# Three up-projection output pairs of phase 0 as two by two steps of seven products

## The chip, the cores and the metric

The kernel runs on one core of one Trainium2 chip. The metric is the time of one execution on the device in microseconds (us), as the median of several runs. Profile times count from the first instruction of the span.

## The reference, cut to what matters

One block of a streaming encoder on x of 512 positions by 1024 channels. The part that the change touches is the channel mixer after the merge:

```python
x = x + (g_conv * y_conv + g_attn * y_attn) @ w_o[l]     # output projection
h = rms_norm(x, norm_ffn_g[l])
up = causal_dwconv(h @ w_up[l], conv_ffn_w[l])           # 1024 -> 2 * 2816
a, b = jnp.split(up, 2, axis=-1)
x = x + (jax.nn.silu(a) * b) @ w_down[l]                 # 2816 -> 1024
```

All operands are float32.

## The kernel before, in words

**Layout and products.** Activations lie transposed, 128 channels on the partitions and the 512 positions along the free axis, so x is 8 blocks of 128 by 512. A weight block is 128 by 128. Each float32 operand is kept as a high part in the type fp32r and a low part, the difference. A product of a weight block and an activation block is three matmul passes (high by high, low by high, high by low), each cut into two halves of 256 positions: six matmuls (`mm3`, whose line is L290). For a chunk of weights, ACT writes the high part (L259) and DVE the low part (L263); both have two buffers (`wh`, `wl`), so a chunk can be split as soon as the chunk before the last one is used up.

**Steps of seven products.** For some matrices the kernel takes two output blocks, two input blocks and the two halves of the positions as a two by two product of blocks, with seven block products where eight would do it the plain way (Winograd's form of Strassen's scheme). Sums of weight blocks and sums of activation blocks ("forms") go in, and four PSUM banks hold the seven products, which are then merged. `seven` runs them, and its matmuls have the line L308. A step of two such doubles takes two chunks: P (768 columns of plain weights, 18 matmuls) and F (1024 columns of weight sums, 24 matmuls). Before the change this is done for five pairs of gates (`GATES`) and for the down projection (`STEPS`).

**Weight sums.** `make_forms` builds the F chunks in device memory, with DMAs alone: copies on SP's queue (L198) and accumulating DMAs on POOL's queue (L201), one wave after another by the calls of `slot()` that the stages make. For the down projection of phase 0 there are six groups, first copied at the start of the output projection.

**Stages.** Projections with attention; gates and merge (`yc`, `ya`, mix chunks, `GATES`), which leaves `mh`/`ml`; output projection (8 chunks `wo0` to `wo7`), whose evacuation adds x (`xr`, 8 DMAs on POOL's queue, L1011 and L1012), scales and splits the sum into `x1h`/`x1l` (L1013, L1014) and adds its squares into `ssq2` on POOL (L966); phase 0 of the channel mixer with the output pairs j = 0 to 11 (`up`, chunks `up0` to `up23`, two per pair), then its steps of the down projection; phase 1 with pairs 12 to 21 and their steps; the last rows and the final norm.

**An up pair.** Two blocks of 48 matmuls, each in one PSUM bank of a ring of six. The norm's factor `rb` is not in `x1h`/`x1l`; it is multiplied in at the evacuation (L1046), since the norm of the whole position is known only after `wo7`. So the matmuls of `up0` and `up1` (`lead`) run ahead of it, with the norm's reduction (`pc_n`) and broadcast (`pb_n`) placed between them. Then come three taps of the convolution (L543 on ACT, L544 and L547 on DVE), silu (L1056, ACT) and the product of the pair (POOL, `ge` at L1061 for even j and `go` at L1068 for odd j). After each odd pair DVE and ACT make the activation forms for the down projection (L1078 to L1088).

**What sets the order.** Matmuls and the listed DMAs keep the order of the program (`keep`). Weight chunks are a single list, `stream`; SP's queue loads them in that order, up to `LOOK` = 7 ahead, into four buffers `raw` (F chunks into `rf`, or into `rg` in the gate stage) as buffers come free. SP's queue is in order: a load that waits holds back all behind it. Work of DVE and ACT that can be put off stands in the list `later`, and after each split `run_later` takes as much of it as a budget in us, set by the chunk's kind, allows.

Of the kernel before, what the change touches and what calls it, by code (L numbers as in the profile page):

```python
# [61 lines left out]
DOUBLES = GATES + STEPS[0] + STEPS[1]  # L62
GROUPS = {"gate": (2, 4, 1), 0: (2, 4, 1), 1: (2, 3, 1)}
# [3 lines left out]
def block_kernel(ctx, tc, xT, vecs, wv, win, wmix, wo, wup, wst, wdp, outT):  # L67
# [168 lines left out]

    def split(hl=None):
# [30 lines left out]
        parts.append((hi, lo))  # L268
        run_later(k, {"u": 1.7, "P": 1.6, "F": 0.75, "i": 3.0, "m": 3.0, "d": 0 if nm == "dp1" else 2.1}.get(nm[0], 3.5))
# [498 lines left out]
    def seven(doubles, n0, sets, operand, goes_on=None, stays=None, done=None):  # L768
# [3 lines left out]
        for n, d in enumerate(doubles):  # L772
            for kind in "PF":
                prods = []
                for s_, (i, q) in enumerate(d):
                    for f, g, b, h in PROD:
                        if (f < 3) == (kind == "P"):
                            wants.setdefault(f"{kind}{n0 + n}", []).append(("q", q))
                            c = 3 * s_ + f if f < 3 else s_ + len(d) * (f - 3)
                            prods.append((c, i, operand(q, g), b, h))  # L780
# [31 lines left out]

    mg = ExitStack()
    mp = mg.enter_context(tc.tile_pool(name="mp", bufs=1))
    pools["rg"] = mp
    mh = mp.tile([P, KB, S], F32R, tag="mh", name="mh")
    ml = mp.tile([P, KB, S], F32R, tag="ml", name="ml")
# [105 lines left out]

    for j in range(KB):
        gs = []
        if j == 0:
# [11 lines left out]
        for pp, hh, ll, o in ((yc, ych, ycl, 0), (ya, oth, otl, 4)):  # L938
            for k in range(4):
# [12 lines left out]
    x1 = xp.tile([P, KB, S], F32, tag="x1", name="x1")  # L952
# [49 lines left out]

    po = None
    make_forms(len(GATES), len(GATES) + len(STEPS[0]), 0)
    for j in range(KB):
# [12 lines left out]
        square_into(ssq2, x1[:, j, :], j == 0, mp, f"sq2_{j}")  # L1018
    mg.close()
    ab.close()  # L1020
# [4 lines left out]
    fp.tile([P, PADL], F32, tag="pad", name="pad_f")  # L1025
# [4 lines left out]
    gh = fp.tile([P, NG, 2 * P], F32R, tag="gh", name="gh")  # L1030
    gl = fp.tile([P, NG, 2 * P], F32R, tag="gl", name="gl")


    acc = ring(*range(6))
# [5 lines left out]
    def up(j, rb2, pu=None):  # L1040
        uu = []
        for s_ in range(2):
            slot()
            p = pu[s_] if pu else block(f"up{2 * j + s_}", x1h, x1l, True)
            z = fp.tile([P, S], F32, tag="fz", name=f"fz{j}{s_}", bufs=2)
            nc.vector.tensor_mul(z, p, rb2)  # L1046
            u = fp.tile([P, S], F32, tag="fu", name=f"fu{j}{s_}", bufs=3)
            taps(u, z, CF + 3 * (2 * j + s_))
            uu.append(u)
        return uu  # L1050

    def glu(ph, j, uu):
# [10 lines left out]
        flush()  # L1063
# [35 lines left out]
    def combine(ph, i, banks, ids):  # L1099
# [5 lines left out]
        def z1():  # L1105
            t["z"] = fp.tile([P, S], F32, tag="fz", name=f"cz{ph}{i}", bufs=2)
# [6 lines left out]
        def u3():  # L1113
            t["u"] = fp.tile([P, S], F32, tag="fz", name=f"cu{ph}{i}", bufs=2)[:, : 2 * P]
# [33 lines left out]
    for ph, (j0, j1) in enumerate(PHASES):  # L1148
        if ph:
            flush()  # L1150
            acc = ring(*X)
        if ph:
            make_forms(len(GATES) + len(STEPS[0]), len(DOUBLES), ph)
        for j in range(j0, j1):
# [11 lines left out]
            glu(ph, j, up(j, nrm["b"], pu))  # L1166
        assert not todo_bg
        seven(
            STEPS[ph], len(GATES) + ph * len(STEPS[0]), ({0: X, 1: Y, 3: X, 2: Y}, {0: X, 1: Y, 2: Y})[ph],
# [39 lines left out]
    yhl = fp.tile([P, 2, 2 * P], F32R, tag="fz", name="yhl", bufs=2)  # L1209
# [62 lines left out]
def _layout(i):  # L1272
# [45 lines left out]
    for w4, d in [(wga, d) for d in GATES] + [(wdn, d) for d in STEPS[0] + STEPS[1]]:  # L1318
# [45 lines left out]
```

## Time and profile before

| | us |
|---|---|
| median of 3 runs (700.04 to 700.89) | 700.57 |
| profiled execution: its own time | 700.14 |
| profiled execution: span, first to last instruction | 697.9 |
| projections and attention, until the first `yc` | 0 to 182.24 |
| gates and merge | 182.24 to 295.18 |
| output projection (`p_wo`) | 295.18 to 338.70 |
| up pairs of phase 0 | 338.70 to 471.20 |
| down projection steps of phase 0 | 471.20 to 528.32 |
| up pairs of phase 1 | 528.32 to 637.12 |
| down projection of phase 1, final norm, output | 637.12 to 697.9 |

The stages are read from the chain of work that ended last, in order of time. In a row of the profile, "x504" counts instructions, a time in ns is the mean of one, and "idle" is what the engine waited just before them, with the engine that ended most of it. PEld is the weight load, which overlaps the matmuls. q1 are DMAs issued by SP, q0 those issued by POOL; "share" is the time of their packets as a share of the 16 DMA engines' time.

### The profile page before, as it was taken

To read this page: it belongs to the slowest core of one execution; us is meant where nothing else is said; L and a number is where in the kernel's file an instruction comes from. 1 tells how busy PE (TensorE), PEld (TensorE's weight loads), DVE (VectorE), ACT (ScalarE), POOL (GpSimd) and SP (SyncE) were. 2 spreads that over 40 slices of the span, in tenths; PEclk is the share of its full clock that TensorE was granted. 3 is DMA by queue.
4 is the path that set the end of the run, shared out by engine and by line. 5 is a ranking of instruction groups with operands and counts; after the bars stand their busy time and mean duration, and the time that the engine had idled before them with its cause. 6 is when DMAs were issued, how large, how long until landed. Compare 5 with 4: busy or idle time off the path is not lost.

```text
span 697.9 us, 14608 instructions
## 1 busy us (share of the span) xinstructions
PE 689.5 (99%) x6008; PEld 688.1 (99%) x6008; DVE 501.1 (72%) x783; ACT 344.4 (49%) x546; POOL 173.3 (25%) x191
## 2 busy tenths in 40 slices
PE   9999999999999999999999999999999999999996
PEld 9999999999999999999999999999999999999995
DVE  6677877776677778754377777778674677878793
ACT  5665655545565444543344444445443344445563
POOL 4134847432200000224504214010000313221001
PEclk9999999999999999999999999999999999999998
DMA  7528989542452555587977855555647696776513
GB/s 254 161 72 274 188 196 206 116 93 86 159 165 81 177 190 177 179 301 149 216 194 168 211 130 128 151 170 166 203 126 231 139 196 157 186 169 178 153 31 121
DMA packets 52690, 116.02 MB, mean 166 GB/s; under 512 B 4960, under 2 KB 23408, under 8 KB 52624
## 3 DMA queue, kind: packets, MB, share of 16 engines
q1 hardware_dynamic: 37464, 94.17, 41.9%
q0 software_dynamic: 13920, 19.74, 17.8%
q10 hardware_dynamic: 1240, 1.19, 0.5%
q8 instruction: 47, 0.77, 0.4%
q14 instruction: 19, 0.16, 0.1%
HBM read 112.92 MB, written 33.03 MB: 209 GB/s over the span
## 4 chain that ended last, share of the span: by engine, by line
PE 97%; DMA 1%; DVE 0%; SPq 0%; ACT 0%; issue 0%; DVEq 0%; ACTq 0%
PE p_up L290 26%; PE dn L308 20%; PE p_in L290 14%; PE p_up L308 8%; PE p_wo L290 6%; PE yc L290 3%; PE ya L290 3%; PE p_q L290 2%; PE p_k L290 2%; PE p_gb L290 2%; PE p_ga L290 2%; PE o L635 2%; PE pa L454 2%; PE pb L456 1%; PE tp L618 1%; PE pdB L290 1%
## 5 line engine op out<-in xcount | busy, mean ns | idle before, releaser
L290 PE MATMUL p_up<-x1h,wl_up 128*128 128x256 f32 x536 | 104.5, 276 | 0.0
L290 PE MATMUL p_up<-x1h,wh_up 128*128 128x256 f32 x536 | 104.4, 276 | 0.0
L290 PE MATMUL p_up<-x1l,wh_up 128*128 128x256 f32 x536 | 104.4, 276 | 0.0
L259 ACT ACTIVATE wh_up<-raw_up 128x1024 fp32r<-128x1024 f32 x44 | 46.7, 1060 | 86.8 <-PE p_up L290 73.4
L290 PEld LDWEIGHTS p_up<-x1h,wl_up 128*128 128x128 f32 x536 | 80.8, 188 | 0.0
L290 PEld LDWEIGHTS p_up<-x1l,wh_up 128*128 128x128 f32 x536 | 80.7, 188 | 0.0
L290 PEld LDWEIGHTS p_up<-x1h,wh_up 128*128 128x128 f32 x536 | 80.6, 188 | 0.0
L263 DVE TENSOR_TENSOR wl_up<-raw_up,wh_up 128x1024 fp32r<-128x1024 f32 x44 | 53.8, 1223 | 20.6 <-ACT wh_up L259 20.6
L1061 POOL TENSOR_TENSOR ge<-fu,fu 128x512 f32<-128x512 f32 x11 | 17.1, 1552 | 161.6 <-DVE fu L547 150.8
L290 PE MATMUL p_in<-xgh,wh_in 128*128 128x256 f32 x288 | 56.8, 279 | 0.0
L290 PE MATMUL p_in<-xgh,wl_in 128*128 128x256 f32 x288 | 56.6, 278 | 0.0
L290 PE MATMUL p_in<-xgl,wh_in 128*128 128x256 f32 x288 | 56.5, 278 | 0.0
L201 POOL DMA_DIRECT2D f<-in_wst_dram x48 | 56.1, 1285 | 0.0
L1046 DVE TENSOR_TENSOR fz<-p_up,rb_n 128x512 f32<-128x512 f32 x44 | 30.3, 690 | 31.6 <-PE p_up L290 31.5
L263 DVE TENSOR_TENSOR wl_F<-raw_F,wh_F 128x1024 fp32r<-128x1024 f32 (+1 forms) x30 | 40.4, 1345 | 12.9 <-ACT wh_F L259 12.8
L290 PEld LDWEIGHTS p_in<-xgh,wh_in 128*128 128x128 f32 x288 | 44.7, 188 | 0.7
L259 ACT ACTIVATE wh_F<-raw_F 128x1024 fp32r<-128x1024 f32 (+1 forms) x30 | 31.5, 1051 | 27.6 <-PE dn L308 24.6
L290 PEld LDWEIGHTS p_in<-xgl,wh_in 128*128 128x128 f32 x288 | 43.7, 188 | 0.0
L290 PEld LDWEIGHTS p_in<-xgh,wl_in 128*128 128x128 f32 x288 | 43.6, 188 | 0.0
L308 PE MATMUL p_up<-x1h,wh_up 128*128 128x256 f32 x168 | 40.3, 277 | 0.0
L308 PE MATMUL p_up<-x1l,wh_up 128*128 128x256 f32 x168 | 40.2, 276 | 0.0
L263 DVE TENSOR_TENSOR wl_in<-raw_in,wh_in 128x1024 fp32r<-128x1024 f32 x26 | 34.2, 1314 | 6.7 <-ACT wh_in L259 6.5
(318 smaller groups left out, 2037.6 us busy)
## 6 DMA issues: line engine op xcount, KB each, us to landing
raw_up<-in_wup_dram SPq DMA_DIRECT2D x44, 512.0 KB, 4.4
raw_F<-f SPq DMA_DIRECT2D x29, 512.0 KB, 4.2
raw_in<-in_win_dram SPq DMA_DIRECT2D x26, 512.0 KB, 3.6
raw_P<-in_wst_dram SPq DMA_DIRECT2D x29, 384.0 KB, 4.0
f<-in_wst_dram POOLq DMA_DIRECT2D x29, 256.0 KB, 5.9
f<-in_wst_dram SPq DMA_DIRECT2D x14, 512.0 KB, 6.3
f<-in_wst_dram POOLq DMA_DIRECT2D x14, 512.0 KB, 8.1
f<-f SPq DMA_DIRECT2D x28, 256.0 KB, 4.0
```

The lines of the kernel that those rows point to most:

```text
L201: return lambda: keep(nc.gpsimd.dma_start(dst, src, accum_op=ALU.add))
L259: ins = nc.scalar.activation(hi, raw, AF.Copy)
L263: ins = nc.vector.tensor_sub(lo, raw, hi.bitcast(F32))
L290: keep(nc.tensor.matmul(out[:, cs], w, x[:, cs], start=start and i == 0 and c == 0, stop=stop and i == 2 and c == len(cut) - 1,))
L308: keep(nc.tensor.matmul(out, wl if x == 1 else wh, xl if x == 2 else xh, start=opens and bk not in seen, stop=closes and bk not in left,))
L454: keep(nc.tensor.matmul(pa[t][:, :VW], xt, w[:, VB:], start=start, stop=stop))
L456: keep(nc.tensor.matmul(pb[t], xt, w[:, :VB], start=start and t % 2 == 0, stop=stop and t % 2 == 1))
L618: keep(nc.tensor.transpose(tp[:, ks], pt[:, ks], ident))
L635: keep(nc.tensor.matmul(o[:, 2 * P * e + c0 : 2 * P * (e + 1)], w, x[:, kb, c0:], start=e == 0 and kb == 0 and i == 0, stop=e == 1 and kb ...
L1046: nc.vector.tensor_mul(z, p, rb2)
L1061: keep(nc.gpsimd.tensor_mul(ge, a.rearrange(halves_of, h=2), b.rearrange(halves_of, h=2)))
```

## The change

The pairs j = 1, 2 and 5 of phase 0 are no longer two plain blocks each but two steps of seven products (`UPD`, P10/F10 to P15/F15 in the stream). Their activation forms are made of x1 times the norm's weight, without the norm's factor, one set for each two blocks of x1, in the output projection stage (`up_forms`, appended to `later`); the factor goes in when the banks are merged (`merge`). Their weight sums are made in the gate and merge stage. The rest makes room for it: x1 is loaded whole in the gate stage by four DMAs in place of the eight `xr`; the arrays of activation forms `gh`/`gl` get a pool of their own that is open earlier; the gate stage's pool lies on the other side; `fz` has four buffers; up evacuations are put into `later` while others wait there; the banks of the up pairs are listed one by one (`turns`); the SBUF reserved for POOL's DMA descriptors is given as 8192 bytes a partition.

```diff
+SUP = (1, 2, 5)
+XF = 26
+UPD = tuple(((j, q), (j, q + 1)) for j in SUP for q in (0, 2))
+DOUBLES = GATES + UPD + STEPS[0] + STEPS[1]
+N0 = len(GATES) + len(UPD)
+GROUPS = {"gate": (2, 4, 1), "up": (2, 4, 1), 0: (2, 4, 1), 1: (2, 3, 1)}
...
-        stream += [(f"up{j}", wup[j], D) for j in range(2 * j0, 2 * j1)]
+        for j in range(j0, j1):
+            if j in SUP:
+                stream += step_chunks(n) + step_chunks(n + 1)
+                n += 2
+            else:
+                stream += [(f"up{i}", wup[i], D) for i in (2 * j, 2 * j + 1)]
...
+        if any(("e",) in w[2] for w in later):
+            run_later(k, {"u": 3.8, "P": 1.6, "F": 1.2}[nm[0]])
+            return
...
+    make_forms(len(GATES), N0, "up")
     for j in range(KB):
         gs = []
+        slot()
+        if j == KB - 1:
+            x1 = xp.tile([P, KB, S], F32, tag="x1", name="x1")
+            for q in range(4):
+                nc.gpsimd.dma_start(x1[:, 2 * q : 2 * q + 2, :], xT[:, 2 * q : 2 * q + 2, :])
...
+        def scale():
+            for b in range(2):
+                kb = 2 * q + b
+                nc.scalar.activation(
+                    y[:, 2 * b : 2 * b + 2, :], x1[:, kb, :].rearrange(halves_of, h=2), AF.Copy, scale=col(G2 + kb)
+                )
+            nc.vector.tensor_sub(b11, b11, b12)
+            nc.vector.tensor_sub(b12, b22, b12)
+
+        def sums():
+            nc.vector.scalar_tensor_tensor(b22, b11, -1.0, b22, op0=ALU.mult, op1=ALU.subtract)
+            nc.vector.scalar_tensor_tensor(b21, b22, -1.0, b21, op0=ALU.mult, op1=ALU.subtract)
+
+        def parts_of():
+            nc.scalar.activation(gh[:, fs, :], y, AF.Copy)
+            nc.vector.tensor_sub(gl[:, fs, :], y, gh.bitcast(F32)[:, fs, :])
+
+        for f, us in ((scale, 0.85), (sums, 0.85), (parts_of, 1.25)):
+            later.append((0, us, (("x", q),), f))
...
-        xr = mt(f"xr{j}")
-        nc.gpsimd.dma_start(xr, xT[:, j, :])
-        nc.vector.tensor_add(x1[:, j, :], p, xr)
+        nc.vector.tensor_add(x1[:, j, :], p, x1[:, j, :])
...
+        if j % 2:
+            up_forms(j // 2)
+    hg.close()
...
+    acc = turns(0, 1, *(2, 3, 4, 5) * 2, 6, 7, 0, 1, 2, 3, 4, 5)
+    USETS = {1: (2, 3, 4, 5), 2: (6, 7, 0, 1), 5: (6, 7, 0, 1)}
...
+        if j in SUP:
+            c = len(GATES) + 2 * SUP.index(j)
             slot()
+            seven(
+                UPD[c - len(GATES) :][:2], c, {j: USETS[j]}, up_form, of="x",
+                done=lambda i, banks, ids: merge(ph, j, banks, ids, rb2, tap, uu),
+            )
+            slot()
+            return
...
+        for f, us, x in (
+            (z1, 0.42, 2), (m1, 0.7, 0), (u3, 0.85, 3), (m2, 0.7, 1),
+            (fin(0), 0.7, None), (lambda: tap(0, gs[0]), 1.4, None),
+            (fin(1), 0.7, None), (lambda: tap(1, gs[1]), 1.4, None),
+            (lambda: glu(ph, j, uu), 0, None),
+        ):
+            later.append((0, us, (ev,) if x is None else (ev, ids[x]), f))
...
-        flush()
+        flush_only([("q", x) for x in range(q)])
```

**SP's queue at the end of the output projection.** `raw_up2` is the weight chunk of `up2`, `f10` and so on are the groups of weight sums, and the brackets name the semaphores that an instruction waits for (DMAHW and DMASW are DMAs of SP and of POOL). Before:

```order
L173 DMA raw_up0_4285<-in_wup_dram 128x1024 [waits DMAHW2_49,DVE_49]
L173 DMA raw_up1_4349<-in_wup_dram 128x1024 [waits DMAHW4_49,DMAHW3_49,DVE_49]
L173 DMA raw_up2_4413<-in_wup_dram 128x1024 [waits DMAHW6_49,DVE_49]
L173 DMA raw_up3_4485<-in_wup_dram 128x1024 [waits DMAHW5_49,DMAHW0_49,DVE_49]
L173 DMA raw_up4_4491<-in_wup_dram 128x1024 [waits DMAHW2_49,DVE_49]
L198 DMA f10_3964<-f10_3964 256x256 [waits DMAHW7_49,DMASW0_49]
L198 DMA f12_3965<-f12_3965 256x256 [waits DMASW1_49]
L198 DMA f14_3966<-f14_3966 256x256 [waits DMAHW1_49,DMASW2_49]
L173 DMA raw_up5_4631<-in_wup_dram 128x1024 [waits DMAHW3_49,DVE_49]
```

The same place in SP's queue with the change (there `f16` to `f20` are the groups that were `f10` to `f14`):

```order
L182 DMA raw_P10_4464<-in_wst_dram 128x768 [waits DMAHW7_49,DVE_49]
L182 DMA raw_F10_4531<-f10_2591 128x1024 [waits DMASW3_49,DMAHW6_49,PE_49,Pool_49]
L182 DMA raw_P11_4533<-in_wst_dram 128x768 [waits DMAHW1_49,DVE_49]
L182 DMA raw_F11_4535<-f10_2591 128x1024 [waits DMAHW0_49]
L182 DMA raw_P12_4547<-in_wst_dram 128x768 [waits DMAHW3_49,DVE_49]
L182 DMA raw_F12_4549<-f12_2592 128x1024 [waits DMAHW2_49,DMASW4_49]
L207 DMA f16_4002<-f16_4002 256x256 [waits DMASW5_49]
L207 DMA f18_4003<-f18_4003 256x256 [waits DMAHW4_49,DMASW6_49]
L207 DMA f20_4004<-f20_4004 256x256 [waits DMAHW5_49,DMASW7_49]
L182 DMA raw_P13_4691<-in_wst_dram 128x768 [waits DMAHW6_49,DVE_49]
L182 DMA raw_F13_4693<-f12_2592 128x1024 [waits DMAHW7_49]
L182 DMA raw_up6_4721<-in_wup_dram 128x1024 [waits DMAHW0_49,DVE_49]
```

Where the next up chunks waited for DVE's splits alone, the first F chunk now waits for PE and POOL too: its buffer lies where `mh`, `ml` and `sq` lay, so it waits for the last matmul of `wo7` and for POOL's last addition into `ssq2`, and all loads behind it wait with it. The load of F13 stands behind that of P13, and P13's waits (DMAHW6) for F10 to have landed.

**DVE's queue from the norm's factor on.** Before, with `fz00`/`fu00` the evacuation and taps of pair 0 and `wl_up2` the low part of a chunk:

```order
L263 TENSOR_TENSOR wl_up2_4634<-raw_up2_4413,wh_up2_4633 128x1024
L263 TENSOR_TENSOR wl_up3_4696<-raw_up3_4485,wh_up3_4695 128x1024
L1046 TENSOR_TENSOR fz00_4613<-p_up0_4497,rb_n2_4609 128x512
L1046 TENSOR_TENSOR fz01_4621<-p_up1_4498,rb_n2_4609 128x512
L544 SCALAR_TENSOR_TENSOR fu00_4615<-fz00_4613,vec_64,fu00_4615 128x511
L544 SCALAR_TENSOR_TENSOR fu01_4623<-fz01_4621,vec_64,fu01_4623 128x511
L547 SCALAR_TENSOR_TENSOR fu00_4615<-fz00_4613,vec_64,fu00_4615 128x510
L547 SCALAR_TENSOR_TENSOR fu01_4623<-fz01_4621,vec_64,fu01_4623 128x510
L1046 TENSOR_TENSOR fz10_4686<-p_up2_4637,rb_n2_4609 128x512
```

The same place of DVE's queue with the change:

```order
L278 TENSOR_TENSOR wl_F10_4724<-raw_F10_4531,wh_F10_4723 128x1024
L1139 TENSOR_TENSOR fz00_4673<-p_up0_4557,rb_n2_4669 128x512
L1139 TENSOR_TENSOR fz01_4681<-p_up1_4558,rb_n2_4669 128x512
L278 TENSOR_TENSOR wl_P11_4752<-raw_P11_4533,wh_P11_4751 128x768
L562 SCALAR_TENSOR_TENSOR fu00_4675<-fz00_4673,vec_64,fu00_4675 128x511
L562 SCALAR_TENSOR_TENSOR fu01_4683<-fz01_4681,vec_64,fu01_4683 128x511
L565 SCALAR_TENSOR_TENSOR fu00_4675<-fz00_4673,vec_64,fu00_4675 128x510
L565 SCALAR_TENSOR_TENSOR fu01_4683<-fz01_4681,vec_64,fu01_4683 128x510
L278 TENSOR_TENSOR wl_F11_4776<-raw_F11_4535,wh_F11_4775 128x1024
L278 TENSOR_TENSOR wl_P12_4804<-raw_P12_4547,wh_P12_4803 128x768
L278 TENSOR_TENSOR wl_F12_4840<-raw_F12_4549,wh_F12_4839 128x1024
L1161 TENSOR_TENSOR uz1_4807<-dn1014_4701,uz1_4807 128x256
```

Between the taps of pair 0 and the first merge (`uz1`) three splits of weights now follow each other, where there was the evacuation of the next plain block.

More of the change, by code (lines that the diff above doesn't have):

```diff
@@ L235, in flush, with flush_only @@
                 later.pop(n)[3]()
+    def flush_only(tags):
+        while n := [n for n, w in enumerate(later) if set(w[2]) & set(tags)]:
+            with after_split():
+                later.pop(n[0])[3]()
     def split(hl=None):
@@ L766, in block_kernel, with seven @@
     open_ = {}
-    def seven(doubles, n0, sets, operand, goes_on=None, stays=None, done=None):
+    def seven(doubles, n0, sets, operand, goes_on=None, stays=None, done=None, of="q"):
         todo, wants = [], {}
```

128 lines of the change are left out of this document (95 added, 33 removed).

## The prediction

> **What bounds the kernel now.** I read the page's busy times and chain first: is one engine the bound, and does it ever wait?
>
> ```profile
> PE 689.5 (99%) x6008; PEld 688.1 (99%) x6008; DVE 501.1 (72%) x783; ACT 344.4 (49%) x546; POOL 173.3 (25%) x191
> ...
> PE 97%; DMA 1%; DVE 0%; SPq 0%; ACT 0%; issue 0%; DVEq 0%; ACTq 0%
> ```
>
> The chain is TensorE nearly throughout, so matmuls taken away are time gained, unless they are replaced by waits. Next, the chain in order of time, for what the matmuls of the touched stage cost:
>
> ```profile
> 220.38 9.52 PE dn L308 x84
> ...
> 338.70 4.76 PE p_up L290 x42
> ...
> 350.50 0.89 PE pb_n L344 x8
> 351.39 1.41 PE p_up L308 x12
> ...
> 362.40 1.36 PE p_up L308 x12
> 363.76 4.08 PE p_up L290 x36
> ...
> 471.20 57.12 PE dn L308 x504
> ```
>
> A plain up block is 12 + 36 = 48 matmuls in 1.36 + 4.08 = 5.44 us, 113.3 ns each. A gate pair in two steps of seven products is 84 in 9.52 us, 113.3 ns as well. The 504 of the down projection show that P and F chunks can follow each other for 57 us without a gap. Then the windows, for the room on the other engines and the clock:
>
> ```profile
> 235.00:250.00 15.00, 15.00 (x135) 15.00 (x134) 11.85 (x16) 7.12 (x10) 1.29 (x1) 1.00 0.49 158
> ...
> 328.00:338.70 10.70, 10.70 (x97) 10.70 (x96) 5.02 (x6) 4.30 (x6) 5.55 (x4) 1.00 0.96 188
> 338.70:352.80 14.10, 14.10 (x127) 14.10 (x126) 5.14 (x7) 5.12 (x7) 4.94 (x4) 1.00 0.95 213
> ...
> 363.70:374.60 10.90, 10.90 (x99) 10.90 (x98) 8.77 (x15) 4.94 (x8) 3.37 (x3) 1.00 0.74 185
> 374.60:385.50 10.90, 10.90 (x99) 10.90 (x98) 7.79 (x11) 5.05 (x8) 3.68 (x3) 1.00 0.73 177
> ```
>
> Columns after the window: PE, PEld, DVE, ACT, POOL busy, then clock, DMA share and GB/s. PE is full in each at clock 1.00. DVE has 5 of 11 us in the output projection and 8.28 of 10.9 in an up pair. The DMA engines are 95% busy from 328 to 352.8, the very place at which the first new chunks must arrive.
>
> **The change part by part.**
>
> *Matmuls.* A transformed pair has two steps of 18 + 24 = 84 matmuls in place of 2 x 48 = 96: 12 x 113.3 ns = 1.36 us less, three pairs **4.08 us**. The passes are of the same kinds and sizes, so I keep the 113.3 ns.
>
> *DVE.* The rows of the operations, mean of one last before the bar of idle time:
>
> ```profile
> L263 DVE TENSOR_TENSOR wl_up<-raw_up,wh_up 128x1024 fp32r<-128x1024 f32 x44 | 53.8, 1223 | 20.6 <-ACT wh_up L259 20.6
> L263 DVE TENSOR_TENSOR wl_F<-raw_F,wh_F 128x1024 fp32r<-128x1024 f32 x29 | 39.7, 1368 | 12.2 <-ACT wh_F L259 12.2
> ...
> L544 DVE SCALAR_TENSOR_TENSOR fu<-fz,vec,fu 128x511 f32<-128x511 f32 x44 | 33.3, 758 | 1.5 <-ACT fu L543 1.5
> ...
> L1046 DVE TENSOR_TENSOR fz<-p_up,rb_n 128x512 f32<-128x512 f32 x44 | 30.3, 690 | 31.6 <-PE p_up L290 31.5
> L263 DVE TENSOR_TENSOR wl_P<-raw_P,wh_P 128x768 fp32r<-128x768 f32 x29 | 27.7, 955 | 10.4 <-ACT wh_P L259 5.9 <-PE dn L308 4.5
> ...
> L861 DVE TENSOR_TENSOR xtl<-xt,xth 128x1024 fp32r<-128x1024 f32 x4 | 4.7, 1219 | 0.1
> ...
> L897 DVE TENSOR_TENSOR ga<-dn,gz 128x512 f32<-128x512 f32 x5 | 3.5, 691 | 0.2
> ...
> L893 DVE TENSOR_TENSOR gz<-dn,gz 128x256 f32<-128x256 f32 x5 | 2.1, 417 | 0.0
> ```
>
> Splits per pair: 2 x (0.96 + 1.37) - 2 x 1.22 = +2.2 us. Merge: three of 256 columns at 0.42, two of 512 at 0.69 and two with the norm's factor at 0.76 make 4.2, less the two `fz` at 0.69: +2.8. So +5.0 us a pair, 13.3 us of DVE work in 9.52 us of matmuls. That would be a new bound if it all had to be done there; but only the splits (4.65 us of the 9.52) must be, and merges and taps stand in `later`. Two pairs push (13.3 - 9.52) x 2 = 7.6 us ahead of them; pairs 3 and 4 have 2 x (10.9 - 8.28) = 5.2 us free, pair 5 pushes 3.8 more, and pairs 6 to 11 have 15.7. The forms (four sets of four operations at 0.42 and one split at 1.22, 11.6 us in all) lie in the output projection, where 43.5 us hold some 23 us of room. I cost DVE at nothing on the path; without that cover it would be 15 + 11.6 us.
>
> The narrowest place is the first transformed pair, where the evacuation of pair 0 falls too. The norm's path is as before, so its matmuls start at 351.39 and need P10, F10, P11, F11, P12 from 351.39, 353.43, 356.15, 358.19 and 360.91; a low part is needed at two thirds of its chunk.
>
> ```profile
> 352.77 1.28 DVE L1046 TENSOR_TENSOR fz<-p_up,rb_n 128x512 f32<-128x512 f32 x2
> ...
> 356.40 1.28 ACT L1056 ACT_TABLE_LOAD   x1 [1.57 <-DVE fu L547]
> 357.69 0.63 ACT L1056 ACTIVATE fu<-fu 128x512 f32<-128x512 f32 x1
> ```
>
> DVE is done with `fz` at 354.05; then the low part of P11 (0.96) and four taps (3.0) stand ahead of that of F11, which ends at 354.05 + 0.96 + 3.0 + 1.37 = 359.4, and is needed at 358.19 + 1.81 = 360.0. ACT's table load waits for the third tap (357.3), and with it, silu and the high part of P12 (0.84, row below) it is at 360.0, needed at 360.91. So 0.6 and 0.9 us are left: nothing lost, and about 0.5 us if an operation there is as slow as the slowest of a row (`wl_F` takes 1.22 to 2.07 in the gate stage). POOL's product `ge` comes after both.
>
> *SP's queue and the DMA engines.* The load of F10 waits for POOL's last square sum:
>
> ```profile
> 313.94 22.09 SPq L173 DMA_DIRECT2D raw_up<-in_wup_dram  x5
> ```
> ```profile
> 341.13 1.79 POOL L966 TENSOR_TENSOR ssq<-ssq,sq 128x512 f32<-128x512 f32 x1 [2.67 <-ACT sq L965]
> ...
> 345.55 2.13 POOL L201 DMA_DIRECT2D f<-in_wst_dram  x2
> ```
> ```profile
> L259 ACT ACTIVATE wh_F<-raw_F 128x1024 fp32r<-128x1024 f32 x29 | 30.9, 1065 | 25.6 <-PE dn L308 22.6 <-PE p_up L290 1.4 <-PE ya L290 0.8
> ...
> L259 ACT ACTIVATE wh_P<-raw_P 128x768 fp32r<-128x768 f32 x29 | 24.4, 842 | 25.2 <-PE dn L308 19.8 <-PE p_up L290 5.4
> ```
>
> Before, five up chunks left SP from 313.94 to 336. Now P10 takes the third place (a block of 5.44 us each, so about 324.8), and F10 not before 342.9; behind it wait P11, F11, P12, F12, three copies of weight sums, P13, F13 and `up6`. Who waits for them: ACT's high parts, and so PE. What each needs (start of its matmuls less ACT's 0.84 or 1.07): F10 352.4, P11 355.3, F11 357.1, P12 360.1, F12 361.9, P13 364.8, F13 366.6, up6 369.4. How fast they come:
>
> ```profile
> q1 hardware_dynamic: 832, 2.70, 42.5%
> ```
> ```profile
> q0 software_dynamic: 846, 1.63, 48.2%
> q1 hardware_dynamic: 2056, 3.48, 44.2%
> ```
> ```profile
> q1 hardware_dynamic: 1275, 2.83, 35.3%
> ```
> ```profile
> DMA to landing us min/median/max: 4.0/5.4/5.6
> ```
> ```profile
> DMA to landing us min/median/max: 3.0/7.0/11.8
> ```
>
> The rows are the queues from 440 to 460, from 338 to 360 and from 320 to 345 (packets, MB, share), then the landing of `raw_up` and of the weight sums from 290 to 375. Alone, q1 moved 2.70 MB in 42.5% of 20 us: 318 GB/s. With POOL's accumulating DMAs beside it I take half, 159, from 345.55 until the last one lands, about 358 (the second of the two leaves near 346, and the slowest landing took 11.8). With 512, 384 and 256 KB a piece, the loads have moved 0.81 MB at 345.55 and 2.79 at 358; with 2.3 us of latency (4.0 less 1.65 for 512 KB) they land at: F10 347, P11 348.5, F11 351.8, P12 354.3, F12 357.6, P13 362.7, F13 364.3, up6 366.0. The smallest margin is **2.1 us at P13**. So nothing is lost, but not by much. Bounds: nothing, and 16.5 us if q1 goes on at the slow 113 GB/s (2.83 MB in 25 us) until `up6`; I take nothing, since that row's loads waited for buffers, not for DMA engines.
>
> The trace bears on a rule here: from 338 to 360 both queues moved at once, at 48.2% and 44.2% of the engines' time. The Trainium skill, "DMA: Bandwidth & Descriptors", section "Queues, rings and completion order", says that each DMA engine takes turns between the queue rows that have work, a packet at a time. By that rule, and the trace agrees, SP's loads can't be shut out by POOL's; but the half lasts as long as POOL has DMAs in flight, which is the first rival below: by the rule the sum is 696.5 if they end near 358, and 698.7 if more follow.
>
> *The rest.* The tile of the F chunks in the gate stage, from 220 to 296 (shortest, median and longest in ns, first and last start):
>
> ```profile
> L259 ACT ACTIVATE wh_F<-raw_F x10: 1066/1067/1069, 220.5 to 284.1; 128x1024 fp32r<-128x1024 f32 x10
> L263 DVE TENSOR_TENSOR wl_F<-raw_F,wh_F x10: 1224/1642/2074, 221.6 to 285.2; 128x1024 fp32r<-128x1024 f32 x10
> L173 SPq DMA_DIRECT2D raw_F<-f x8: 326/327/327, 223.7 to 271.5; - x8
> ```
>
> Three groups of weight sums, 2.1 MB each, come on top of a DMA share of 0.49 there: at 160 GB/s 39 us of 113, so about 0.35 more. The last load leaves at 271.5 for a split at 284.1, 12.6 us ahead, and none of the idle time that the rows of `wh_P` and `wh_F` name was ended by a DMA. The four loads of x1 take the place of eight; they stand on POOL's queue ahead of the merge addition of pair 2, with its inputs ready about 5 us sooner. Nothing, or 1 us if cover fails. In the down projection and the tail, PE's rows are as before.
>
> **Sum.** 700.14 - 4.08 = 696.06 us for the profiled execution. That execution is 0.43 below the median shown, so the median becomes 700.57 - 4.08 = **696.5 us**.
>
> **The rivals.**
>
> *SP's loads share the engines to the end.* The groups' second additions follow the first, so q1 stays at 159 GB/s after 358. Then P13 lands at 365.0, F13 at 368.3, `up6` at 371.6: 0.2, 1.6 and 2.2 us late. PE waits 2.2 us: 698.7. For it: share 0.95 to 352.8. Against: the share falls to 0.74 after 363.7.
>
> *The loads are late by more than the gain.* Same place, q1 at 113 GB/s: `up6` (4.59 MB from 343) lands at 385.9, 16.5 late, and the time is 713. It decides from about 163 GB/s on, where `up6` is 4.1 late. For it: before, q1 moved 158 GB/s from 338 to 360. Against: that was all that it was asked for, as PE had no wait.
>
> *The change doesn't do what it says*: the splits run behind DVE's merges, a chunk here and there waits about as much as it saves (1.36 us a pair): 700.6. Against: the gate stage has DVE at 11.85 of 15 us with the same merges and no gap of PE.
>
> **How the numbers follow.** Chances: the forecast 0.63 (own range 695.8 to 697.3), shared engines or a wait of DVE of up to 2.6 us 0.20 (to 699.1), no gain 0.05, late loads 0.12. About 0.2% (1.4 us) is what a measurement of this kernel can tell from no change. Faster by that: 0.63 + 0.20 - 0.02 for the edge = 0.81. Within: 0.07. Slower: 0.12. The range, 695.8 to 699.4, holds the first two cases; below it there is nothing, since PE is full in all that is touched.
>
> **What would show it.** Right: 5972 matmuls in place of 6008; in the chain, `dn` x168 in 19.04 us from 351.39, then `up6`; ACT's idle time before `wh_F` and `wh_P` ended by PE. Wrong: a DMA as the releaser of `wh_P`, `wh_F` or `wh_up` between 352 and 370 (the loads), `wl` ended late behind taps near 360 (DVE), or a gap of PE in the gate stage (weight sums).

## The result, and the profile after

| | kernel before | changed kernel |
|---|---|---|
| median of 12 runs each | 700.49 us (700.01 to 700.89) | 697.99 us (697.21 to 700.40) |
| ratio, 95% interval | | 0.9969 (0.9961 to 0.9977) |
| profiled execution: own time, span | 700.14, 697.9 us | 698.61, 696.8 us |

The change is faster by 2.5 us, with the sign forecast and inside the range, but 1.6 us of the forecast 4.08 are missing. Its times also scatter over 3.2 us where those of the kernel before scatter over 0.9. The profiled execution lies 0.6 above its median, so what it shows of losses is on the large side.

The page of the changed kernel: the span, the engines, and the two DMA queues (packets, MB, share of the 16 engines).

```profile
span 696.8 us, 14636 instructions
...
PE 686.7 (99%) x5972; PEld 684.9 (98%) x5972; DVE 530.9 (76%) x824; ACT 359.7 (52%) x567; POOL 180.7 (26%) x196
...
q1 hardware_dynamic: 40776, 99.68, 44.0%
q0 software_dynamic: 16304, 22.88, 20.6%
```

The 36 matmuls are gone: 5972 for 6008. The chain of waits at the transformed pairs (start, length, what):

```profile
353.50 19.12 PE dn L326 x168
372.62 1.36 PE p_up L326 x12
...
394.38 9.52 PE dn L326 x84
```

Four steps stand without a gap in 19.12 us, where the forecast had 19.04, and two in 9.52, which is its pitch of 113.3 ns. Nothing is lost where the prediction saw the danger. It is lost in two other places. First the gate stage, PE and then the queue of ACT (columns: start, length, instruction; in brackets the idle time before it and what ended it):

```profile
269.60 0.50 PE L326 MATMUL dn<-xth,wl_F 128*128 128x256 f32 x3
271.65 0.38 PE L326 MATMUL dn<-xgh,wh_P 128*128 128x256 f32 x1 [1.55 <-ACT wh_P L274]
```
```profile
265.43 1.07 ACT L274 ACTIVATE wh_F<-raw_F 128x1024 fp32r<-128x1024 f32 x1 [0.18 <-ACT gb L937]
270.24 0.63 ACT L978 ACTIVATE mh<-ga 128x512 fp32r<-128x512 f32 x1 [3.75 <-POOL ga L977]
270.77 0.83 ACT L274 ACTIVATE wh_P<-raw_P 128x768 fp32r<-128x768 f32 x1
```

After the last three matmuls (269.60 + 3 x 0.113 = 269.94) PE stands until 271.65: **1.7 us**. It waits for the high part of the second P chunk of gate column 6. That one was free to go, but stands on ACT behind `mh` of column 5, and `mh` waited 3.75 us for POOL. POOL's queue:

```profile
251.25 1.30 POOL L977 TENSOR_TENSOR ga<-ga,gb 128x512 f32<-128x512 f32 x1 [10.43 <-DVE gb L976]
267.84 1.04 POOL L210 DMA_DIRECT2D f<-in_wst_dram  x1 [15.29 <-DMA f<-f]
268.44 1.76 POOL L977 TENSOR_TENSOR ga<-ga,gb 128x512 f32<-128x512 f32 x1
```

POOL computed nothing for 15.29 us. It stood in front of one accumulating DMA of the new weight sums, which needs a copy to have landed; the sum of two products of column 5 (L977), all the gate needs from POOL, stands behind it. For the most part that cost nothing, since the sum's last input came late:

```profile
265.45 0.69 DVE L976 TENSOR_TENSOR gb<-gb,ya 128x512 f32<-128x512 f32 x1
```

It was ready at 265.45 + 0.69 = 266.14. The DMA was issued at 267.84 and the sum started at 268.44, 2.3 us after it could have. The Trainium skill, "DMA: Bandwidth & Descriptors", section "SWDGE vs HWDGE vs iDMA", says that a transfer that adds into its destination can only be issued from GpSimd; the trace agrees in that all 57 issues of L210 are POOL's (page: busy, mean ns, idle time before):

```profile
L210 POOL DMA_DIRECT2D f<-in_wst_dram x57 | 66.1, 1311 | 15.6 <-DMA f<-f 15.3
```

So these sums share one queue with whatever POOL computes.

The second place is the seam of phase 0, where the down projection begins. PE, then DVE's queue with the last up chunk's split, what stands next and last, and the first P chunk's split:

```profile
470.26 0.28 PE L326 MATMUL dn<-gl,wh_P 128*128 128x256 f32 x1
471.32 0.50 PE L326 MATMUL dn<-gh,wl_P 128*128 128x256 f32 x2 [0.78 <-DVE wl_P L278]
```
```profile
459.43 1.51 DVE L278 TENSOR_TENSOR wl_up<-raw_up,wh_up 128x1024 fp32r<-128x1024 f32 x1 [1.04 <-ACT wh_up L274]
460.87 0.74 DVE L562 SCALAR_TENSOR_TENSOR fu<-fz,vec,fu 128x511 f32<-128x511 f32 x1
...
469.12 1.28 DVE L1231 TENSOR_TENSOR gl<-go,gh 128x512 fp32r<-128x512 f32 x2
470.32 0.95 DVE L278 TENSOR_TENSOR wl_P<-raw_P,wh_P 128x768 fp32r<-128x768 f32 x1
```

The step between the two groups of matmuls is 1.06 us where it is 0.11 elsewhere: **0.95 us** lost. Between the two splits DVE works 9.5 us without a break on deferred evacuations, taps and forms (460.87 to 470.32). In the kernel before, the same pair of splits:

```profile
461.45 1.23 DVE L263 TENSOR_TENSOR wl_up<-raw_up,wh_up 128x1024 fp32r<-128x1024 f32 x1 [0.40 <-ACT wh_up L259]
...
466.68 0.96 DVE L263 TENSOR_TENSOR wl_P<-raw_P,wh_P 128x768 fp32r<-128x768 f32 x1 [0.19 <-ACT wh_P L259]
```

Theories that the experiments had to tell apart. For the gate stage: the **queue theory** (order on POOL's queue, as above) against the **DMA theory** (the traffic of the sums, whose share of the DMA engines from 215 to 296 rose as the rows below show, delays loads). For the seam: the **budget theory** (DVE has room, but is told to do too little of the deferred work after each up chunk) against the **load theory** (three pairs are too much for it). Windows before and after (PE, PEld, DVE, ACT, POOL, clock, DMA share, GB/s):

```profile
215.00:296.00 81.00, 81.00 (x717) 81.00 (x716) 62.63 (x81) 38.26 (x49) 8.66 (x9) 1.00 0.50 163
...
404.00:476.00 72.00, 72.00 (x637) 72.00 (x637) 53.91 (x79) 33.59 (x47) 14.92 (x12) 1.00 0.53 142
```
```profile
215.00:296.00 81.00, 79.45 (x701) 79.25 (x700) 60.41 (x79) 36.30 (x46) 14.86 (x15) 1.00 0.74 218
...
404.00:476.00 72.00, 71.22 (x628) 71.02 (x627) 68.10 (x102) 37.77 (x56) 20.34 (x14) 1.00 0.55 143
```

### The profile page after: what moved, and what is told of

Read it like the earlier page. It is cut to its first block, busy times and chain, and to the rows that moved or that the text cites. A ratio compares the mean times of both kernels' runs of the same rounds, so it can differ in the third digit from the quotient of the medians.

```text
span 696.8 us, 14636 instructions
## 1 busy us (share of the span) xinstructions
PE 686.7 (99%) x5972; PEld 684.9 (98%) x5972; DVE 530.9 (76%) x824; ACT 359.7 (52%) x567; POOL 180.7 (26%) x196
## 4 chain that ended last, share of the span: by engine, by line
PE 58%; DVE 2%; DMA 0%; ACT 0%; issue 0%; DVEq 0%; ACTq 0%
PE p_up L308 21%; PE dn L326 19%; PE p_up L326 7%; PE p_wo L308 6%; PE pdB L308 1%; PE pdA L308 1%; PE ya L308 1%; PE yc L308 1%; DMA raw_dp<-in_wdp_dram 0%; PE pc_n L343 0%; DVE fu L562 0%; DVE fu L565 0%; PE pb_n L362 0%; DVE gl L1231 0%; DVE wl_up L278 0%; DVE x L1384 0%
## 5 line engine op out<-in xcount | busy, mean ns | idle before, releaser
L308 PE MATMUL p_up<-x1h,wh_up 128*128 128x256 f32 x464 | 90.5, 276 | 0.0
L308 PE MATMUL p_up<-x1l,wh_up 128*128 128x256 f32 x464 | 90.3, 276 | 0.0
L308 PE MATMUL p_up<-x1h,wl_up 128*128 128x256 f32 x464 | 90.3, 276 | 0.0
L210 POOL DMA_DIRECT2D f<-in_wst_dram x57 | 66.1, 1311 | 15.6 <-DMA f<-f 15.3
L308 PEld LDWEIGHTS p_up<-x1h,wh_up 128*128 128x128 f32 x464 | 69.9, 188 | 0.0
L308 PEld LDWEIGHTS p_up<-x1l,wh_up 128*128 128x128 f32 x464 | 69.9, 188 | 0.0
L308 PEld LDWEIGHTS p_up<-x1h,wl_up 128*128 128x128 f32 x464 | 69.8, 188 | 0.0
L274 ACT ACTIVATE wh_P<-raw_P 128x768 fp32r<-128x768 f32 (+1 forms) x36 | 30.0, 834 | 31.4 <-PE dn L326 22.6
L326 PE MATMUL dn<-gh,wh_F 128*128 128x256 f32 x192 | 45.1, 276 | 0.0
L326 PE MATMUL dn<-gl,wh_F 128*128 128x256 f32 x192 | 45.1, 276 | 0.0
L278 DVE TENSOR_TENSOR wl_P<-raw_P,wh_P 128x768 fp32r<-128x768 f32 (+1 forms) x36 | 34.5, 958 | 13.6 <-ACT wh_P L274 9.0
```

The source lines that it names most:

```text
L210: return lambda: keep(nc.gpsimd.dma_start(dst, src, accum_op=ALU.add))
L274: ins = nc.scalar.activation(hi, raw, AF.Copy)
L278: ins = nc.vector.tensor_sub(lo, raw, hi.bitcast(F32))
L308: keep(nc.tensor.matmul(out[:, cs], w, x[:, cs], start=start and i == 0 and c == 0, stop=stop and i == 2 and c == len(cut) - 1,))
L326: keep(nc.tensor.matmul(out, wl if x == 1 else wh, xl if x == 2 else xh, start=opens and bk not in seen, stop=closes and bk not in left,))
```

## The experiments

All times are medians of five runs or more, each set with the kernel before on the same chip; where two kernels were on different chips, their differences to the kernel before are compared.

### 1. x1's loads written behind the last sums

Why does that DMA stand where it does? It is the third accumulation for pair 5. In the program it is written in column 7 and pinned behind the POOL instruction written just ahead of it. That is a load of x1, which is pinned to nothing and went off early:

```profile
215.56 2.16 POOL L953 DMA_DIRECT2D x<-in_xT_dram  x4 [7.75 <-DVE xtl L883]
```

The accumulation was thereby free to be placed ahead of the sum of column 5. The edit moves the loads behind the sums; on POOL this one accumulation changes its place and nothing else does.

```diff
     for j in range(KB):
         gs = []
         slot()
-        if j == KB - 1:
-            x1 = xp.tile(...); four loads
...
+        if j == KB - 1:
+            x1 = xp.tile(...); four loads
         if j >= GJ:
             split_next()
```

> One edit on the changed kernel: the four loads of x1 are written behind the last three sums of the gate stage instead of ahead of them. On POOL exactly one instruction moves: the third accumulation of the group of pair 5, which stood ahead of the gate product sum of column 5, stands behind that of column 6. All transfers stay. Queue theory (POOL waited 15.3 us for a copy with the gate sum behind it, ACT's mh behind that and wh_P behind mh): PE's gap of 1.7 us at 269.8 is gone, the median falls by 0.5 to 1.7 us from 698.0, and the scatter of the runs shrinks towards the 0.9 us of the kernel before. DMA theory (the extra 6 MB of the gate stage make a load late): the gap stays within 0.5 us of 1.7, the time stays within 0.3. Both leave the gap of 1.0 us at 470.

Measured: 696.86 us (696.46 to 697.12); before 700.50; ratio 0.9948 (0.9935 to 0.9960). POOL and ACT in the same stretch:

```profile
266.22 1.30 POOL L977 TENSOR_TENSOR ga<-ga,gb 128x512 f32<-128x512 f32 x1 [13.66 <-DVE gb L976]
267.45 1.04 POOL L210 DMA_DIRECT2D f<-in_wst_dram  x1
```
```profile
267.55 0.64 ACT L978 ACTIVATE mh<-ga 128x512 fp32r<-128x512 f32 x1 [1.05 <-POOL ga L977]
268.09 0.83 ACT L274 ACTIVATE wh_P<-raw_P 128x768 fp32r<-128x768 f32 x1
```

The sum now starts as soon as DVE has its input, 2.2 us earlier, and the high part 2.7 earlier. PE has no gap there: the window 215 to 296 is full again with the same traffic:

```profile
215.00:296.00 81.00, 81.00 (x717) 81.00 (x716) 62.74 (x81) 38.20 (x49) 14.85 (x15) 1.00 0.74 223
```

Share 0.74 as in the changed kernel, gap gone: the queue theory holds and the DMA theory falls. The median is 1.1 lower and the runs lie within 0.7 us. So the scatter, too, came from here: how long POOL stands hangs on when a copy lands, and in the traces of the changed kernel and of experiments 1, 2 and 4 this copy landed 6.4 to 7.6 us after its issue. The later kernels agree: those that keep the wait (experiments 2 and 4) scatter over 1.8 and 2.0 us in five runs, those without it over 0.5 to 0.8 (experiments 3 and 5 to 8).

### 2. More deferred work per up chunk

```diff
-            run_later(k, {"u": 3.8, "P": 1.6, "F": 1.2}[nm[0]])
+            run_later(k, {"u": 4.6, "P": 1.6, "F": 1.2}[nm[0]])
```

> One edit on the changed kernel: after each up chunk's split VectorE may run 4.6 us of deferred work instead of 3.8 while evacuations are deferred. Budget theory (VectorE has room in phase 0, but 3.8 us per chunk hardly drains what is deferred, and all that is left stands ahead of the first low part of the down projection): the gap of 1.0 us at 470 is gone and the median falls by 0.9 to 1.0 us. Load theory (three transformed pairs are simply too much work for VectorE in phase 0): the gap stays within 0.3 us of 1.0, or comes back as gaps before other splits, and the time stays. The gate stage's gap stays, about 0 to 3 us from run to run.

Measured: 697.83 us (696.59 to 698.34), ratio 0.9958 (0.9946 to 0.9971). The seam's gap is gone, but a step of 0.6 us before a low part of an up chunk has come at 447.8, so half of the gain is given back. The median hides even that, because the gate stage's gap is still there and varies. POOL and PE once more:

```profile
268.17 1.76 POOL L977 TENSOR_TENSOR ga<-ga,gb 128x512 f32<-128x512 f32 x1
```
```profile
271.38 0.39 PE L326 MATMUL dn<-xgh,wh_P 128*128 128x256 f32 x1 [1.37 <-ACT wh_P L274]
```

From POOL's sum to PE's next matmul it is 271.38 - 268.17 = 3.21 us; in the changed kernel 271.65 - 268.44 = 3.21 as well. On the seam: the budget theory is right on the place, and neither theory on the time.

### 3. Both

The diffs of experiments 1 and 2 together.

> Both edits at once: x1's loads behind the sums, and 4.6 us of deferred work. If the matmul term of 4.08 us was right and the two gaps are all that it lost, the median is 4.0 to 4.1 us below the kernel before: about 696.4, with no gap of PE over 0.4 us between 165 and 660. If a seven-product pair saves less than 1.36 us, or a third loss exists, it stays above 697.

Measured: 696.49 us (696.06 to 696.86), ratio 0.9942 (0.9930 to 0.9955): 4.0 us below the kernel before. Only the gap at 446.7 is left, about 0.5 us; the row of waits (engine and line, what it waited for, us in total, times, longest):

```profile
PEld p_up L326 <- DVE wl_up L278: 0.6, 1, 0.6
```

The time was as forecast, but "no gap over 0.4" was missed by this one.

### 4. The dose the other way

Two accumulations slip ahead of the sum of column 5:

```diff
         gs = []
-        slot()
         if j == KB - 1:
             x1 = xp.tile(...); four loads
+        slot()
```

> The dose the other way: x1's loads one place earlier, so that two accumulations (of the groups of pairs 2 and 5) stand on POOL ahead of the gate product sum of column 5 instead of one. Transfers as in the changed kernel. Queue theory: one more issue of 0.6 to 1.0 us stands ahead of the gate sum, so PE's gap grows from 1.7 to about 2.3 to 2.8 us and the median rises by 0.5 to 1.0 us to about 698.5 to 699.0. DMA theory: no change in gap or time (within 0.3 us).

Measured: 697.66 us (697.19 to 699.16), ratio 0.9964 (0.9950 to 0.9977). The expected rise did not come:

```profile
265.51 1.04 POOL L210 DMA_DIRECT2D f<-in_wst_dram  x1 [12.45 <-DMA f<-f]
267.18 1.03 POOL L210 DMA_DIRECT2D f<-in_wst_dram  x1 [0.63 <-issue]
267.76 1.76 POOL L977 TENSOR_TENSOR ga<-ga,gb 128x512 f32<-128x512 f32 x1
```
```profile
270.97 0.39 PE L326 MATMUL dn<-xgh,wh_P 128*128 128x256 f32 x1 [0.38 <-ACT wh_P L274]
```

The second issue passed while POOL would have waited for the later copy anyway: that copy, issued at 259.86, took 6.5 us to land (266.4), and the DMA that needs it starts 0.8 behind that, as in the changed kernel (267.0 and 267.84). So this was no larger dose, and its time tells nothing of the two theories. The link to PE is again 270.97 - 267.76 = 3.21 us. Three executions with three starts of the sum give the same distance, and the first experiment shows that without a wait the distance no longer matters.

### 5. Both, with 5.0 us

On the version of experiment 1:

```diff
-            run_later(k, {"u": 3.8, "P": 1.6, "F": 1.2}[nm[0]])
+            run_later(k, {"u": 5.0, "P": 1.6, "F": 1.2}[nm[0]])
```

> As the version with both edits, with 5.0 us of deferred work after an up chunk's split in place of 4.6. With 4.6 one gap of 0.5 us was left at 446.7, where 6.6 us of VectorE's work (by the rows' durations) stood between two splits behind three stretches of 5.0; with 5.0 the stretch of 6.6 comes behind stretches of 4.4, 4.6 and 3.7. Backlog theory: that gap shrinks below 0.3 us, none comes at the down projection, and the median is 0.2 to 0.5 below 696.5. Rival (a larger budget only moves the wait): another gap of 0.3 to 1.0 us in 353 to 470, or at the first low part of pair 5, and the median stays at 696.5 or above.

Measured: **695.57 us** (695.39 to 696.03); before 700.14; ratio 0.9935 (0.9921 to 0.9948). No matmul from 165 us on starts more than 0.3 us after its turn. DVE at the seam, and its window:

```profile
459.37 1.23 DVE L278 TENSOR_TENSOR wl_up<-raw_up,wh_up 128x1024 fp32r<-128x1024 f32 x1 [0.51 <-ACT wh_up L274]
...
463.64 1.45 DVE L278 TENSOR_TENSOR wl_P<-raw_P,wh_P 128x768 fp32r<-128x768 f32 x1
```
```profile
404.00:476.00 72.00, 72.00 (x638) 72.00 (x637) 64.83 (x95) 35.87 (x52) 17.45 (x11) 1.00 0.50 141
```

The same work over the whole program (DVE 530.2 us on this kernel's page, 530.9 in the changed kernel) sits earlier: 64.83 us in this window instead of 68.10. The load theory falls for three pairs. This version beats both kernels.

### 6. Two pairs

```diff
-SUP = (1, 2, 5)
+SUP = (1, 2)
...
-    acc = turns(0, 1, *(2, 3, 4, 5) * 2, 6, 7, 0, 1, 2, 3, 4, 5)
+    acc = turns(0, 1, *(2, 3, 4, 5, 6, 7) * 2, 0, 1, 2, 3, 4, 5)
```

on the version of experiment 1, with 3.8 us.

> The version with x1's loads behind the sums, with pairs 1 and 2 alone as steps of seven products; pair 5 is an ordinary pair again, and the order of the PSUM banks after pair 2 follows. 5984 matmuls. Cost theory (each pair saves 12 matmuls, 1.36 us; the gap at the down projection comes from what pair 5 pushes back on VectorE): no gap near 470, median 700.5 - 0.4 - 2.72 = 697.4, that is 0.5 above the version with three pairs, which has 1.36 more saved and 0.95 of gap. Rival (the gap comes from pairs 1 and 2, or from deferring as such): the gap of 1.0 stays, and the median is 698.3.

Measured: 697.41 us (697.02 to 697.55); before 700.14; ratio 0.9959 (0.9947 to 0.9971). That is 2.73 us for two pairs, where the matmuls make 2.72; the interval (2.0 to 3.7 us) is far wider than this agreement. PE has no gap near 470: with 3.8 us per chunk, two pairs' work drains and the third's does not. Whether the number of pairs counts here, or that pair 5 stands closer to the seam, this run does not tell.

### 7. A load more on SP's queue

```diff
             else:
+                if nm == "P13":
+                    extra = dr.tile([P, 2 * D], F32, tag="extra", name="extra")
+                    keep(nc.sync.dma_start(extra[:, :D], wst[0, :, :D]))
                 keep(nc.sync.dma_start(raw[:, :ncol], ...))
```

> The version with x1's loads behind the sums, plus one DMA of 512 KB on SP's queue (weights copied to a place in DRAM that nobody reads) just ahead of the load of P13. It leaves the computation alone. By the prediction's working P13 lands 2.1 us before it is needed, and a load of 512 KB there takes 3.3 us at 159 GB/s (1.6 at 318). Narrow-margin theory: P13 lands 1.2 us late, PE shows a gap of 1.0 to 1.6 us near 365 whose releaser is ACT's wh_P behind a DMA, and the median rises by as much to about 698.2. Rival (the DMA engines had room to spare, so the margin never mattered): no gap there, median within 0.3 us of 696.9.

Measured: 697.16 us (696.97 to 697.51), ratio 0.9957 (0.9944 to 0.9969). The high part of P13, first in experiment 1's kernel, then here, and PE here:

```profile
362.84 0.85 ACT L274 ACTIVATE wh_P<-raw_P 128x768 fp32r<-128x768 f32 x1 [1.16 <-DMA raw_P<-in_wst_dram]
```
```profile
365.09 0.85 ACT L277 ACTIVATE wh_P<-raw_P 128x768 fp32r<-128x768 f32 x1 [2.90 <-DMA raw_P<-in_wst_dram]
```
```profile
365.99 0.50 PE L329 MATMUL dn<-gh,wl_F 128*128 128x256 f32 x3
366.33 0.28 PE L329 MATMUL dn<-x1h,wh_P 128*128 128x256 f32 x1
```

The two executions do not stand at the same times. This one is 0.5 us later well before the place (the first matmul of the output projection is at 295.61, against 295.10 in experiment 1's kernel), and so it is at the place itself. In experiment 1's kernel:

```profile
365.81 0.28 PE L326 MATMUL dn<-x1h,wh_P 128*128 128x256 f32 x1
```

Of the 2.25 us between the two high parts 0.52 are thus the execution's, and the load delayed P13 by 1.7 us, not by 3.3. The high part is done at 365.94 and PE takes it at 366.33, in its turn: 0.4 us are left. In experiment 1's kernel it was done at 363.69 for 365.81, a margin of 2.1, as the prediction had it. So ACT does wait for the DMA, PE does not: no gap there, as the rival says. The medians alone would not settle it: 697.16 is 0.3 above 696.86, and by the differences to the kernel before (2.98 and 3.64 us) 0.7, which the intervals do not part. The margin was small, as the narrow-margin theory says, but its price for a load was too high: 1.7 us is near the 1.6 that it gave for 318 GB/s.

The half that the prediction gave SP's queue beside POOL's DMAs can be read as well. The queues from 345.8 to 358.2 in experiment 1's kernel (packets, MB, share):

```profile
q1 hardware_dynamic: 913, 2.43, 60.0%
q0 software_dynamic: 480, 0.95, 41.3%
```

SP's queue moved 2.43 MB in 12.4 us, 196 GB/s and not 159. POOL's last accumulation of this group, issued at 346.4, landed 14.8 us later, near 361.3 and not near 358.

### 8. Four pairs

On the version of experiment 5:

```diff
-SUP = (1, 2, 5)
+SUP = (1, 2, 4, 6)
...
-    acc = turns(0, 1, *(2, 3, 4, 5) * 2, 6, 7, 0, 1, 2, 3, 4, 5)
-    USETS = {1: (2, 3, 4, 5), 2: (6, 7, 0, 1), 5: (6, 7, 0, 1)}
+    acc = turns(0, 1, 2, 3, 0, 1, 6, 7, 0, 1, 6, 7, 2, 3, 4, 5)
+    USETS = {1: (2, 3, 4, 5), 2: (6, 7, 0, 1), 4: (4, 5, 6, 7), 6: (2, 3, 4, 5)}
```

> The best version so far (x1's loads behind the sums, 5.0 us of deferred work per up chunk) with four pairs, 1, 2, 4 and 6, in place of 1, 2 and 5, and PSUM banks given out for that. 5960 matmuls; a fourth group of weight sums in the gate stage. Matmul theory (VectorE still has room, 5.0 us a pair in a stage where it had some 29 us free): another 1.36 us, median 694.2, no gap of PE over 0.3 us. Backlog theory (VectorE or SP's loads are now the bound in phase 0): gaps that sum to 1 us or more between 353 and 475, median at 695.2 or above.

Measured: 697.60 us (696.97 to 697.71); before 700.10; ratio 0.9961 (0.9948 to 0.9973). Two us slower than three pairs in place of 1.4 faster. The windows' row and the two waits of PE:

```profile
404.00:476.00 72.00, 69.78 (x613) 69.39 (x612) 67.54 (x101) 39.26 (x58) 19.18 (x12) 1.00 0.52 144
```
```profile
PE dn L326 <- ACT wh_F L274: 1.6, 1, 1.6
...
PE p_up L326 <- DVE wl_up L278: 0.6, 1, 0.6
```

PE loses 2.2 us, as the backlog theory says. That DVE has too little room for four pairs is not shown by this: it is busy 67.54 of 72 us, and the changed kernel had 68.10 with a loss that went when the work was handed out differently. Four pairs with another limit were not run. The larger wait is ACT's: its `wh_F` at 469.48 stands behind a silu that waited 2.76 us for taps on DVE.

### 9. to 11. What lies around the span

Own time less span was 2.2 us in the kernel before (2.18 to 2.29 in the nine runs of experiments 1 to 4) and about 1.8 in every kernel with the change. Three kernels looked for the reason. On the kernel before, the scratch of POOL's DMAs alone, which the change sets in its last line:

```diff
-    nc = _bacc.Bacc("TRN2", target_bir_lowering=False, num_devices=1)
+    nc = _bacc.Bacc("TRN2", target_bir_lowering=False, num_devices=1, dynamic_dma_scratch_size=8192)
```

> One argument on the kernel before, from the last line of the change: the scratch of the descriptors of POOL's DMAs is set to 8192 as the kernel is created. No instruction moves. The runs so far show own time less span of 2.1 to 2.3 us for the kernel before and 1.75 to 1.82 for every kernel with the change. Outside-the-span theory (this argument shortens what lies around the program): span 697.8 to 698.7 as before, own time less span 1.8, median 0.4 below the kernel before, about 700.1. Rival (the 0.4 us comes from something else in the change, such as its instructions): no difference, 700.5.

The change without pairs, on the version of experiment 1:

```diff
-SUP = (1, 2, 5)
+SUP = ()
...
-        if j % 2:
+        if j % 2 and SUP:
             up_forms(j // 2)
...
-    acc = turns(0, 1, *(2, 3, 4, 5) * 2, 6, 7, 0, 1, 2, 3, 4, 5)
+    acc = turns(*(0, 1, 2, 3, 4, 5) * 4)
```

> The rest of the change without its steps: no output pair is transformed, no forms of x1 and no weight sums for pairs are made; left are the four early loads of x1, the pools that were moved, the longer-lived tiles of forms and the scratch of POOL's DMAs. 6008 matmuls. What is asked is where the 0.4 us outside the span come from (own time less span: 2.2 in the kernel before, 1.8 in all kernels with the change; the scratch alone left 2.2). Layout theory: own time less span is 1.8 here, span as before, median about 0.4 below the kernel before. Step theory (it comes with the steps, their sums or their chunks): own time less span is 2.2 and the median equals that of the kernel before within 0.2.

And x1's loads alone, on the kernel before (the four loads stand in column 7 of the gate stage):

```diff
+        if j == KB - 1:
+            x1 = xp.tile(...); four loads
...
-        xr = mt(f"xr{j}")
-        nc.gpsimd.dma_start(xr, xT[:, j, :])
-        nc.vector.tensor_add(x1[:, j, :], p, xr)
+        nc.vector.tensor_add(x1[:, j, :], p, x1[:, j, :])
```

> One part of the change alone on the kernel before: x is read by four loads into x1 in the gate stage in place of eight loads of 256 KB in the output projection, and added in place. The version without pairs had 0.4 us less outside the span and 0.3 less inside it behind the last instructions, and the scratch alone had neither. Load theory (what shrinks is bound to the number or the buffers of POOL's loads): own time less span is 1.8 and the median 0.4 to 0.7 below the kernel before. Pool theory (it is bound to the moved pools and tiles, which this kernel leaves as they were): own time less span stays 2.2 and the median within 0.2 of the kernel before.

Measured:

| | median | kernel before | ratio | own time less span |
|---|---|---|---|---|
| scratch alone | 700.30 | 700.14 | 1.0000 (0.9991 to 1.0009) | 2.17 to 2.25 |
| no pairs | 699.41 | 700.10 | 0.9991 (0.9982 to 1.0001) | 1.77 to 1.88 |
| x1's loads alone | 700.00 | 700.11 | 0.9995 (0.9986 to 1.0004) | 1.78 to 1.88 |

The scratch does nothing. The 0.4 us outside the span follow x1's loads (their number, place and buffers changed together, and no run parts these), but no saving of the time as a whole is shown. With the loads alone the span is 698.1 to 698.4 in 9 of 11 runs; that of the kernel before on the same chip is 697.7 to 697.9 in 8 of 15 runs and 698.2 to 698.5 in the other 7. Whether the span grew by what was lost outside, or these runs merely fell more often at the later of the two places, stays open. For the change without pairs a gain of 0.7 us is measured with an interval that just holds none; it stays open.

## Why the prediction was right, and what it missed

- **Matmul term, 4.08 us: right.** 36 matmuls fewer at an unchanged pitch. Freed of both gaps, the same 5972 matmuls are 700.14 - 695.57 = 4.57 us below the kernel before. The 0.5 beyond 4.08 is not clear of noise (the interval is 3.6 to 5.5 us); what the version without pairs may have on its own (0.7, interval to none) could be in it, though the 2.73 us of the two pairs show none of it.
- **SP's queue and the DMA engines, nothing: right, its working in part by luck.** P13 was to land at 362.7 with 2.1 us to spare; in experiment 1's kernel its high part starts at 362.84 on a DMA's landing, and 2.1 are left. But errors cancel in it: SP's queue was faster beside POOL's DMAs than the half (196 GB/s for 159), those lasted 3 us longer, and the first load, F10, landed at 349.5 where 347 was worked out. Both rivals on late loads fall: from 353 on, PE shows no gap in the transformed pairs. A DMA as releaser of `wh_P` there had been named as a sign against the forecast. The changed kernel doesn't show it, experiment 1's does, and experiment 7 shows that this row alone proves no loss.
- **Narrowest place, 0.6 and 0.9 us left: right** in that nothing was lost in the 19.12 us of the first two pairs. There was more room than worked out: in experiment 1's kernel the low part of F11 and the high part of P12 were both done 1.2 us ahead of their matmuls.
- **"Nothing, or 1 us if cover fails" for the gate stage: the step that failed.** The DMA half of it was sound: share up by 0.24 where 0.35 was forecast, no load late. What failed is the sentence on POOL's queue. It followed x1's loads to the instruction behind them, and not the accumulation that is pinned to them and travelled along. Price: 1.7 us in the profiled execution; the median fell by 1.1 when it was undone.
- **DVE at nothing on the path: failed at the seam, 0.95 us.** "Pairs 6 to 11 have 15.7 free" holds as far as it was needed: in experiment 5 the same work leaves no wait. But the work is handed out after each chunk's split by a limit of 3.8 us, what has been put off keeps new evacuations behind it, and the rest falls due in one piece ahead of the first low part of the down projection. The forecast counted room and not how the program may use it.
- **"In the down projection PE's rows are as before": wrong for the same reason.**
- **The rival "splits run behind DVE's merges"** had the right engine and the wrong place: no split inside the pairs was late, the one behind twelve pairs was. With four pairs the split of an up chunk was late too (0.6 us).

In the two profiled executions 4.08 - 1.7 - 0.95 = 1.4 us should be left, and 700.14 - 698.61 = 1.5 were measured. By medians, 2.5 measured, 1.1 and 0.95 make 4.55 for the 4.57 of the clean version; that this fits to 0.02 is luck, since the intervals are wider than 1 us.

## What to carry to other kernels

A queue that runs in order carries its waits over to all that stands behind: when DMAs that wait for other DMAs share it with arithmetic, read for each of them what it waits for and which result is queued behind, and pin them to something that stays in place. Room summed over a stage is only a bound; look for the rule that hands the work out and for the point at which the rest falls due. And when a kernel's runs scatter more than those of the kernel it came from, look for a wait on a landing that has come onto the path.

## What was not expected of the hardware

- An accumulating DMA that waits for a copy held POOL for 15.29 us, the last 1.7 of them with a sum ready behind it; a copy of 256 KB, the last of three issued from 257.5 to 259.4, released it only at 267.8.
- A DRAM-to-DRAM transfer of 512 KB, put on SP's queue while POOL's accumulations were in flight, moved the landing behind it by 1.7 us: some 300 GB/s, about what both queues moved together there (301 GB/s from 349 to 365), and not the half of 159 that the forecast gave SP's queue.
- The time outside the span fell from 2.2 to 1.8 us when eight loads on POOL's queue became four that stand earlier, without a measurable change of the whole. So the spans of two kernels are not to be compared as if they were times.
